# Ten instead of seven seven-product groups, with running results kept in PSUM, in a four-branch decoder layer on one Trainium2 core

## The chip, the cores and the metric

The kernel runs as one program on 1 core of one Trainium2 chip. Its time is the device time of one execution in microseconds (us); the figure quoted is the median over runs. One execution is recorded by the hardware profiler; its rows give start, duration and waits of every instruction on TensorE (PE; PEld is its weight load), VectorE (DVE), ScalarE (ACT), GpSimd (POOL) and on the DMA queue of SyncE (SP).

## The reference, cut to what matters

One layer with a batch of 1, 256 tokens and a model width of 2048, all in float32. The input is normalised and projected to some 22,900 columns; four branches of width 1024 (two masked attentions, a short convolution, a cross-attention) follow; each branch's result is gated and projected, weighted by a sigmoid gate of the input, and summed; one output projection and a final norm follow.

```
xn = rms_norm(x, ln_g)
(a_q, a_k, a_v, a_g, c_b, c_c, c_h, c_g, s_q, s_k, s_v, s_g, m_q, m_g,
 i_q, i_k, i_w, r_a, r_c, r_s, r_m) = [xn @ w for w in cols]
...
y_m = memory_attention(...) * silu(m_g)          # and y_a, y_c, y_s in the same way
merged = (sigmoid(r_a) * (y_a @ w_branch[0]) + sigmoid(r_c) * (y_c @ w_branch[1])
          + sigmoid(r_s) * (y_s @ w_branch[2]) + sigmoid(r_m) * (y_m @ w_branch[3]))
out = rms_norm(x + merged @ w_out, final_g)
```

The gates r_a, r_c, r_s, r_m are each a product of 256 tokens x 2048 by 2048 x 2048; so is the output projection.

## The kernel before, in words

**Three matmuls for one.** Every float32 weight is split into `hi` (a rounded copy, made by ACT) and `lo` (the rest, a subtraction on DVE), and the activations are kept in the same two parts; one exact product is hi*hi + hi*lo + lo*hi, that is three matmuls in the fast float32r form (`products`, `products_t`). A block of 1024 weight columns per partition thus costs one ACT cast (L104) and one DVE subtraction (L105), and 12 matmuls of 512 columns where both halves of the tokens use it. `hi` and `lo` rotate over 4 buffers each; raw weights come by 1 MB DMAs on the SP queue into 4 `raw` buffers.

**Two kinds of projection.** `project_t` keeps weights as the stationary operand and streams the 256 tokens of `x_hl` (256 columns per matmul, tiles `acc`). `project` keeps 128 tokens stationary and streams 512 weight columns, for token half 0 and 1 in turn (tiles `r`, `w`, `v`, `o`): 16 chunks of 128 inputs x 2 token halves x 3 = 96 matmuls for 512 output columns.

**By halves.** Two neighbouring blocks of 512 output columns need 192 matmuls by `project`. `by_halves` takes the first 8 of the 16 input chunks as a 2 x 2 block product (2 token halves, 2 groups of 4 chunks, 2 column blocks) and forms it with seven products instead of eight (the Strassen-Winograd form); the other 8 chunks are added plainly. A product is 4 chunks x 3 = 12 matmuls, so a group has 180. The weights' differences (`b12 - b11` and so on) are made by DVE, in place in the raw tiles; sums of token blocks (`x_sums`) are made once by `sums_of`. In the group before, the products `m1`, `m5`, `m6`, `m7` go to PSUM banks of their own and DVE joins them in SBUF (L248, L249, L254, L255); eight PSUM reads by DVE in all. A scheduler fixes one order of instructions per engine before the program runs; at run time each engine goes through its list in order and waits on semaphores.

**Where groups are used.** Memory branch M, selection branch S, attention branch A: the second half (`j = 1`) of the branch's gate columns; convolution branch C: both halves; and the value projections S_V and A_V: seven groups. The other three gate halves and the output projection go by `project`. The order of work is: M, indexer, S (S_Q, S_K, S_V, attention beside S_G, gates and branch products), A in the same way, C, output blocks 0 to 4 (512, 512, 512, 256, 256 columns) and the final norm.

**Where tiles stand.** Pools are laid one after the other in each partition. Counting the tile sizes in that order, `x_hl` starts 32 bytes past a multiple of 256, `x_sums` too; `y`, `raw`, `hi` and `lo` start 96 bytes past one.

Of the kernel before, what the change touches and what calls it, by code (L numbers as in the profile page):

```python
# [9 lines left out]
F32 = mybir.dt.float32  # L10
# [5 lines left out]
P = 128  # L16
# [21 lines left out]
SECTIONS_N = [(S_V, W), (A_V, W), (R_0, 4 * D)]  # L38
# [6 lines left out]
TOPK = 64  # L45


@with_exitstack
def hybrid_kernel(ctx, tc, x, xT, mem, memT, ln_g, mem_ln_g, w_t, w_n, w_idx, conv_w, conv_b, w_mem_k, w_mem_v,
# [26 lines left out]
    cb = const.tile([P, 8], F32, name="cb")  # L76
    nc.gpsimd.dma_start(out=g_x, in_=ln_g)
# [79 lines left out]
    def products(o, ah, al, hi, lo, start, stop):  # L157

        nc.tensor.matmul(o, lhsT=ah, rhs=hi, start=start, stop=False)  # L159
        nc.tensor.matmul(o, lhsT=ah, rhs=lo, start=False, stop=False)  # L160
        nc.tensor.matmul(o, lhsT=al, rhs=hi, start=False, stop=stop)  # L161
# [60 lines left out]
    def by_halves(srcs, act, sums, nat, done):  # L222
# [3 lines left out]
        (n00, n10), (n01, n11) = ([part(nat, t, n) for t in range(2)] for n in range(2))  # L226

# [5 lines left out]

        b11 = quarter(srcs[0], 0)
# [30 lines left out]
        product(y, a(1, 0), b21, True, False)
        for k0 in (8, 12):
            plain((y, x), act, srcs[0], k0, (False, False), (k0 == 12,) * 2)
        for t, (o, i) in enumerate(((n00, y), (n10, x))):
            nc.vector.tensor_add(o, i, o)
            done(t, 0, o, False)  # L270
# [26 lines left out]
    def columns(c0, nat, done, halved, srcs=None):  # L297
# [416 lines left out]
```

## Time and profile before

| | |
|---|---|
| median of 3 runs | 1399.0 us (1398.69 to 1400.92) |
| the profiled execution's own time | 1398.06 us |
| its span, first to last instruction | 1396.3 us |
| PE busy | 1380.4 us, 99% of the span |
| DVE busy | 933.4 us, 67% |
| ACT busy | 729.2 us, 52% |
| granted TensorE clock, mean | 0.997 of full speed |

The span leaves 1.8 us of the profiled execution's time outside. Matmuls overlap in the pipeline, so PE counts as busy even where they follow each other more slowly than they could; the distance from one matmul's start to the next tells more than the busy share.

### The profile page before, as it was taken

What the parts mean: (1) busy time and instruction counts of PE and PEld (TensorE: products, weight loads), DVE (VectorE), ACT (ScalarE), POOL (GpSimd) and SP (SyncE); (2) the same over time, 40 slices, a digit from 0 to 9 for tenths busy, and PEclk for the clock granted to TensorE, in tenths of its full rate; (3) what the DMA queues carried; (4) which work ended last, traced back from release to release, by engine and by line L of the source; (5) the groups of instructions that cost most, each with busy time, mean ns of one, the idle gap of its engine ahead of it and who ended that gap; (6) DMA issues with size and microseconds to landing.
All of it is one profiled execution on the core that took longest, in us unless ns stands there. A gap on an engine that the chain in (4) does not pass through costs nothing.

```text
span 1396.3 us, 21263 instructions
## 1 busy us (share of the span) xinstructions
PE 1380.4 (99%) x8796; PEld 1243.9 (89%) x8796; DVE 933.4 (67%) x1123; ACT 729.2 (52%) x991; POOL 11.0 (1%) x25
## 2 busy tenths in 40 slices
PE   9999999999999999999999999999999999999997
PEld 9998998789998898878999899878999998878887
DVE  7687764774848884596546885487547558787654
ACT  7663675453445684354445585445343345545443
POOL 1000000000000000000000000000000000000000
PEclk9999999999999999999999999999999999999999
DMA  9774545375554735537553746537555654736551
GB/s 343 291 271 173 191 156 180 128 266 189 172 197 133 254 128 183 189 135 247 188 193 133 243 150 211 182 125 266 183 181 187 225 192 148 265 130 241 183 197 73
DMA packets 49969, 269.49 MB, mean 193 GB/s; under 512 B 6656, under 2 KB 17456, under 8 KB 19024
## 3 DMA queue, kind: packets, MB, share of 16 engines
q1 hardware_dynamic: 48960, 264.03, 55.0%
q0 software_dynamic: 624, 3.31, 0.6%
q8 instruction: 69, 1.13, 0.3%
q10 hardware_dynamic: 288, 0.79, 0.1%
q14 instruction: 28, 0.23, 0.0%
HBM read 265.88 MB, written 2.10 MB: 192 GB/s over the span
## 4 chain that ended last, share of the span: by engine, by line
PE 85%; DVE 8%; DMA 3%; issue 2%; ACT 2%; SPq 0%; POOLq 0%; POOL 0%; DVEq 0%; ACTq 0%
PE acc L138 13%; PE acc L140 13%; PE acc L139 13%; DVE lo L105 5%; PE w L160 4%; PE w L161 4%; PE w L159 4%; PE r L159 4%; PE r L161 4%; PE r L160 4%; PE o L160 2%; PE o L161 2%; PE o L159 2%; DMA raw<-in_w_n 1%; PE y L160 1%
## 5 line engine op out<-in xcount | busy, mean ns | idle before, releaser
L105 DVE TENSOR_TENSOR lo<-raw,hi 128x1024 fp32r<-128x1024 f32 (+1 forms) x538 | 640.0, 1202 | 416.5 <-ACT hi L104 414.4
L104 ACT CAST hi<-raw 128x1024 fp32r<-128x1024 f32 (+1 forms) x538 | 552.2, 1032 | 547.8 <-PE acc L139 196.4
L139 PE MATMUL acc<-x_hl,hi 128*128 128x256 f32 x1520 | 426.0, 280 | 0.0
L138 PE MATMUL acc<-x_hl,hi 128*128 128x256 f32 x1520 | 425.4, 280 | 0.5 <-ACT qt L155 0.5
L140 PE MATMUL acc<-x_hl,lo 128*128 128x256 f32 x1520 | 425.8, 280 | 0.0
L140 PEld LDWEIGHTS acc<-x_hl,lo 128*128 128x128 f32 x1520 | 288.1, 190 | 0.1
L138 PEld LDWEIGHTS acc<-x_hl,hi 128*128 128x128 f32 x1520 | 284.8, 187 | 0.9 <-ACT qt L155 0.7
L139 PEld LDWEIGHTS acc<-x_hl,hi 128*128 128x128 f32 x1520 | 284.8, 187 | 0.2
L159 PE MATMUL w<-hi,y 128*128 128x512 f32 x256 | 99.9, 390 | 0.0
L161 PE MATMUL w<-hi,y 128*128 128x512 f32 x256 | 99.7, 389 | 0.0
L160 PE MATMUL w<-lo,y 128*128 128x512 f32 x256 | 99.6, 389 | 0.0
L159 PE MATMUL r<-hi,x_hl 128*128 128x512 f32 x248 | 98.3, 396 | 0.0
L161 PE MATMUL r<-hi,x_hl 128*128 128x512 f32 x248 | 97.9, 395 | 0.0
L160 PE MATMUL r<-lo,x_hl 128*128 128x512 f32 x248 | 97.6, 394 | 0.0
L159 PEld LDWEIGHTS w<-hi,y 128*128 128x128 f32 x256 | 48.1, 188 | 10.0
L161 PEld LDWEIGHTS w<-hi,y 128*128 128x128 f32 x256 | 48.1, 188 | 10.0
L160 PEld LDWEIGHTS w<-lo,y 128*128 128x128 f32 x256 | 48.1, 188 | 9.9
L161 PEld LDWEIGHTS r<-hi,x_hl 128*128 128x128 f32 x248 | 46.7, 188 | 10.6
L160 PEld LDWEIGHTS r<-lo,x_hl 128*128 128x128 f32 x248 | 46.7, 188 | 10.4
L159 PEld LDWEIGHTS r<-hi,x_hl 128*128 128x128 f32 x248 | 46.9, 189 | 10.2
L161 PE MATMUL o<-hi,mt 128*128 128x512 f32 (+1 forms) x160 | 55.3, 347 | 0.0
L160 PE MATMUL o<-lo,mt 128*128 128x512 f32 (+1 forms) x160 | 55.1, 346 | 0.0
(246 smaller groups left out, 1860.7 us busy)
## 6 DMA issues: line engine op xcount, KB each, us to landing
raw<-in_w_t SPq DMA_DIRECT2D x92, 1024.0 KB, 5.0
raw<-in_w_n SPq DMA_DIRECT2D x80, 1024.0 KB, 4.9
raw<-in_w_branch SPq DMA_DIRECT2D x32, 1024.0 KB, 5.3
raw<-in_w_out SPq DMA_DIRECT2D x16, 1024.0 KB, 4.8
raw<-in_w_mem_k SPq DMA_DIRECT2D x8, 1024.0 KB, 6.4
raw<-in_w_mem_v SPq DMA_DIRECT2D x8, 1024.0 KB, 5.5
raw<-in_w_t SPq DMA_DIRECT2D x16, 256.0 KB, 5.9
raw<-in_memT SPq DMA_DIRECT2D x2, 1024.0 KB, 8.8
```

The costliest lines, as they stand in the source:

```text
L104: nc.scalar.copy(out=hi, in_=src)
L105: nc.vector.tensor_sub(out=lo, in0=src, in1=hi.bitcast(F32))
L138: nc.tensor.matmul(o, lhsT=hi, rhs=a[:, 0], start=(k == 0), stop=False)
L139: nc.tensor.matmul(o, lhsT=hi, rhs=a[:, 1], start=False, stop=False)
L140: nc.tensor.matmul(o, lhsT=lo, rhs=a[:, 0], start=False, stop=(k == nk - 1))
L159: nc.tensor.matmul(o, lhsT=ah, rhs=hi, start=start, stop=False)
L160: nc.tensor.matmul(o, lhsT=ah, rhs=lo, start=False, stop=False)
L161: nc.tensor.matmul(o, lhsT=al, rhs=hi, start=False, stop=stop)
```

## The change

It does five things. (1) `by_halves` is rewritten: the bank `u` takes the product a11*b11, is copied out by ACT (L253), goes on accumulating s1*h1, is copied out again (L265), goes on with s2*h2, is copied out a third time (L268), and then takes the plain part; bank `m` likewise takes s0*h1, is copied (L260) and goes on. DVE adds only four times at the end (`finish`, L247), ACT copies four times instead of once. (2) The weight differences go to tiles `held` of their own, in the room of `kt` and `vv` for gates and of `y` elsewhere; raw tiles are no longer overwritten. (3) The gates of S and A at `j = 0` and output blocks 1 and 2 become groups: ten in all; the output pair needs sums of `mt`, made by one more `sums_of` (two raw buffers, `m_sums` in the room of `x_sums`). (4) Tiles move: a 224-byte tile `fill`, 256 more bytes in each `hi` and `lo` tile, and 448 more in `u` put `x_hl`, `x_sums`, `mt`, `y`, `raw`, `hi` and `lo` on multiples of 256 bytes; a `hi` or `lo` used as the stationary operand begins 64 bytes later. (5) `yt` has one buffer instead of two.

```
+STATIONARY = 64
+    fill = const.tile([P, 56], F32, name="fill")
+    nc.gpsimd.memset(fill, 0.0)
...
-    def parts_tiles(w=NB, c=NB):
-        return [spl.tile([P, 2 * NB], F32R, name=n, tag=n).rearrange("p (k c) -> p k c", c=w)[:, :, :c]
-                for n in ("hi", "lo")]
+    def parts_tiles(w=NB, c=NB, place=0):
+        i = place // 4
+        return [spl.tile([P, 2 * NB + 64], F32R, name=n, tag=n)[:, i:i + 2 * NB]
+                .rearrange("p (k c) -> p k c", c=w)[:, :, :c] for n in ("hi", "lo")]
...
-                hi, lo = parts_tiles(w, c)
+                hi, lo = parts_tiles(w, c, STATIONARY if w == TB else 0)
...
-    def by_halves(srcs, act, sums, nat, done):
+    def by_halves(srcs, act, sums, nat, done, room):
...
+        held = [big.tile([P, 8 // len(room) * NB], F32, name="held", tag=r) for r in room]
+        h1, h2 = (v.rearrange("p (k c) -> p k c", c=NB) for v in
+                  (held if len(room) == 2 else (held[0][:, :4 * NB], held[0][:, 4 * NB:])))
...
         b11 = quarter(srcs[0], 0)
-        m1 = bank("m", tag)
-        product(m1, a(0, 0), b11, True, True)
-        nc.scalar.copy(out=n00, in_=m1)
-        z, r = bank("z", other), bank("r", other)
-        plain((z, r), act, srcs[1], 8, (True, True), (False, False))
+        u = bank("u", tag)
+        product(u, a(0, 0), b11, True, True)
+        nc.scalar.copy(out=n00, in_=u)
+        x, y = bank("x", other), bank("y", other)
+        plain((y, x), act, srcs[0], 8, True, False)
         b12 = quarter(srcs[1], 0)
-        nc.vector.tensor_sub(out=b11, in0=b12, in1=b11)
-        m5 = bank("m", tag)
-        product(m5, s(0), b11, True, True)
+        nc.vector.tensor_sub(out=h1, in0=b12, in1=b11)
+        m = bank("m", tag)
+        product(m, s(0), h1, True, True)
+        nc.scalar.copy(out=n11, in_=m)
+        plain((y, x), act, srcs[0], 12, False, False)
         b22 = quarter(srcs[1], 4)
-        nc.vector.tensor_sub(out=b11, in0=b22, in1=b11)
-        m6 = bank("m", tag)
-        product(m6, s(1), b11, True, True)
-        nc.vector.tensor_add(n10, m6, n00)
-        nc.vector.tensor_add(n01, m5, n10)
-        plain((z, r), act, srcs[1], 12, (False, False), (False, True))
-        nc.vector.tensor_sub(out=b12, in0=b22, in1=b12)
-        m7 = bank("m", tag)
-        product(m7, s(2), b12, True, True)
-        nc.vector.tensor_add(n10, m7, n10)
-        nc.vector.tensor_add(n11, m7, n01)
-        product(z, s(3), b22, False, True)
...
+        nc.vector.tensor_sub(out=h1, in0=b22, in1=h1)
+        product(u, s(1), h1, False, True)
+        nc.scalar.copy(out=n01, in_=u)
+        nc.vector.tensor_sub(out=h2, in0=b22, in1=b12)
+        product(u, s(2), h2, False, True)
+        nc.scalar.copy(out=n10, in_=u)
+        product(m, s(3), b22, False, False)
+        plain((m, u), act, srcs[1], 8, False, False)
         b21 = quarter(srcs[0], 4)
...
+        nc.vector.tensor_sub(out=h1, in0=b21, in1=h1)
+        product(x, a(1, 1), h1, False, True)
+        finish(x, 1, 0)
+        plain((m, u), act, srcs[1], 12, False, True)
+        product(y, a(1, 0), b21, False, True)
+        finish(m, 0, 1)
+        finish(u, 1, 1)
+        finish(y, 0, 0)
...
-    finish(BR_S, S_G, q, (False, True))
+    finish(BR_S, to_gate(S_G, q))
...
-    finish(BR_A, A_G, q, (False, True))
+    finish(BR_A, to_gate(A_G, q))
...
+    sums_of(lambda k0, n: mt[:, k0:k0 + n], m_sums[0])
...
+        yield from block(0)
+        got = []
+        nat = nat_tile("no")
+        by_halves([w_out[1], w_out[2]], lambda k: mt[:, k], m_sums[0], nat,
+                  lambda t, n, src, psum: got.append((1 + n, t, src)), ("y",))
+        yield from got
+        for n in range(3, last + 1):
+            yield from block(n)
```

The order that the scheduler fixes, at three places, all in the gate group of branch S at `j = 1`. First PE, before: the end of product `m5` (its bank is `m_5988`) and the beginning of `m6` (`m_6012`).

```order
L161 MATMUL m_5988<-hi_5999,x_sums_1518 128x512
L159 MATMUL m_5988<-hi_5999,x_sums_1518 128x512
L160 MATMUL m_5988<-lo_6000,x_sums_1518 128x512
L161 MATMUL m_5988<-hi_5999,x_sums_1518 128x512
L159 MATMUL m_6012<-hi_6013,x_sums_1518 128x512
L160 MATMUL m_6012<-lo_6014,x_sums_1518 128x512
L161 MATMUL m_6012<-hi_6013,x_sums_1518 128x512
```

The two products that need fresh differences stand side by side there. PE after, at the second and third products that bank `u` takes (`u_5950`); `m_6011` is bank `m`:

```order
L167 MATMUL u_5950<-lo_6081,x_sums_1520 128x512
L168 MATMUL u_5950<-hi_6080,x_sums_1520 128x512
L166 MATMUL m_6011<-hi_6113,x_sums_1520 128x512
L166 MATMUL u_5950<-hi_6092,x_sums_1520 128x512
L167 MATMUL u_5950<-lo_6093,x_sums_1520 128x512
L168 MATMUL u_5950<-hi_6092,x_sums_1520 128x512
L166 MATMUL u_5950<-hi_6092,x_sums_1520 128x512
```

One matmul for bank `m` now stands between the last one that adds s1*h1 to `u` and the first that adds s2*h2; the two plain runs stand ahead, one on either side of s0*h1.

DVE before, around the difference that `m6` needs (L245); `lo_6014` and `lo_6024` are its rests, and L499 adds up branch products of the gate half before:

```order
L499 TENSOR_TENSOR merged_2561<-merged_2561,sig_5495 128x512
L105 TENSOR_TENSOR lo_5990<-raw_5925,hi_5989 128x1024
L105 TENSOR_TENSOR lo_6000<-raw_5925,hi_5999 128x1024
L499 TENSOR_TENSOR merged_2561<-merged_2561,sig_5495 128x512
L245 TENSOR_TENSOR raw_5925<-raw_6009,raw_5925 128x2048
L105 TENSOR_TENSOR lo_6014<-raw_5925,hi_6013 128x1024
L105 TENSOR_TENSOR lo_6024<-raw_5925,hi_6023 128x1024
```

The difference L245 reads the tile that `lo_6000` has just read, and `lo_6014` follows it at once. DVE after, at the same step (L263 is the difference that L245 was, L266 the one for h2):

```order
L266 TENSOR_TENSOR held_5947<-raw_6067,raw_6008 128x2048
L110 TENSOR_TENSOR lo_6013<-held_5946,hi_6012 128x1024
L110 TENSOR_TENSOR lo_6023<-held_5946,hi_6022 128x1024
L110 TENSOR_TENSOR lo_6036<-raw_6033,hi_6035 128x1024
L263 TENSOR_TENSOR held_5946<-raw_6067,held_5946 128x2048
L110 TENSOR_TENSOR lo_6052<-raw_6033,hi_6051 128x1024
L110 TENSOR_TENSOR lo_6071<-held_5946,hi_6070 128x1024
L110 TENSOR_TENSOR lo_6081<-held_5946,hi_6080 128x1024
L110 TENSOR_TENSOR lo_6093<-held_5947,hi_6092 128x1024
L272 TENSOR_TENSOR held_5946<-raw_6167,held_5946 128x2048
```

The rests for s0*h1 (`lo_6013`, `lo_6023`) and a plain block now stand ahead of the difference L263, one plain block behind it, and h2 is made earlier. ACT after, around the second copy (L265) and the third (L268) out of `u_5950`; the other rows are casts:

```order
L109 CAST hi_6092<-held_5947 128x1024
L109 CAST hi_6102<-held_5947 128x1024
L109 CAST hi_6113<-raw_6067 128x1024
L265 COPY sig_5945<-u_5950 128x512
L109 CAST hi_6123<-raw_6067 128x1024
L109 CAST hi_6135<-raw_6133 128x1024
L268 COPY sig_5945<-u_5950 128x512
L109 CAST hi_6151<-raw_6133 128x1024
```

One cast stands ahead of the second copy, two between it and the third.

## Rows read from the trace of the kernel before

**Rows 1.** The page: span, busy time of the engines, the granted TensorE clock in 40 slices.

```profile
span 1396.3 us, 21263 instructions
PE 1380.4 (99%) x8796; PEld 1243.9 (89%) x8796; DVE 933.4 (67%) x1123; ACT 729.2 (52%) x991; POOL 11.0 (1%) x25
...
PEclk9999999999999999999999999999999999999999
```

**Rows 2.** Busy time by stretch: the seven groups, each from its first matmul to the first of the next stage. Columns: start and end, length, busy time and instruction count of PE, PEld, DVE, ACT, POOL, granted clock, DMA share, GB/s.

```profile
261.30:304.05 42.75, 41.90 (x182) 33.52 (x181) 37.68 (x35) 23.97 (x25) 0.00 (x0) 1.00 0.60 207
432.88:476.01 43.13, 42.91 (x194) 35.04 (x193) 38.32 (x40) 26.54 (x32) 0.00 (x0) 1.00 0.60 208
598.46:643.61 45.15, 43.59 (x181) 34.79 (x180) 38.99 (x37) 24.36 (x25) 0.00 (x0) 0.96 0.58 198
755.83:798.99 43.16, 42.94 (x195) 35.04 (x194) 38.21 (x40) 26.52 (x32) 0.00 (x0) 1.00 0.60 207
921.38:965.28 43.90, 42.27 (x182) 33.49 (x180) 38.80 (x37) 23.99 (x25) 0.00 (x0) 1.00 0.59 203
1167.96:1210.39 42.43, 42.09 (x182) 33.50 (x181) 37.36 (x35) 26.12 (x29) 0.53 (x1) 1.00 0.67 236
1233.06:1276.38 43.32, 42.38 (x182) 33.42 (x180) 38.16 (x36) 23.98 (x25) 0.00 (x0) 1.00 0.60 208
sum 303.84, PE 298.07 PEld 238.80 DVE 267.52 ACT 175.47 POOL 0.53; mean PE 42.58 PEld 34.11 DVE 38.22 ACT 25.07 POOL 0.08
```

**Rows 3.** The same view of the three stretches that become groups: the gate of S at `j = 0`, that of A, and output blocks 1 and 2.

```profile
531.88:576.68 44.80, 44.80 (x194) 36.30 (x193) 20.83 (x18) 20.49 (x23) 0.00 (x0) 1.00 0.55 182
854.80:899.60 44.80, 44.80 (x194) 36.30 (x193) 20.82 (x18) 20.50 (x23) 0.00 (x0) 1.00 0.60 205
1322.81:1366.76 43.95, 43.95 (x194) 36.06 (x192) 24.42 (x25) 19.31 (x24) 0.00 (x0) 1.00 0.52 177
```

**Rows 4.** The same view of four other stretches: a branch product of S (tiles `w`, 96 matmuls of 512 columns), and three stretches of `project_t` (256 columns): most of S_Q and S_K (576 matmuls), A_Q and A_K (768), C_C to C_G (1,536).

```profile
576.68:598.46 21.78, 21.78 (x97) 18.02 (x96) 13.78 (x13) 9.03 (x10) 0.00 (x0) 1.00 0.48 166
367.60:432.88 65.28, 65.28 (x578) 65.28 (x577) 40.23 (x58) 28.90 (x38) 0.00 (x0) 1.00 0.54 186
665.37:755.83 90.46, 90.46 (x770) 90.45 (x769) 43.89 (x39) 38.05 (x49) 0.00 (x0) 1.00 0.53 181
987.05:1167.96 180.91, 180.91 (x1538) 180.91 (x1536) 100.96 (x115) 73.94 (x83) 0.54 (x1) 1.00 0.55 189
```

**Rows 5.** The instructions in order of time around the end of `m5` in the S group. Columns: start, duration, engine, line and operation; in brackets the idle time before and what ended it.

```profile
606.92 2.28 DVE L245 TENSOR_TENSOR raw<-raw 128x2048 f32<-128x2048 f32 x1
...
609.23 0.39 PE L161 MATMUL m<-hi,x_sums 128*128 128x512 f32 x1
609.32 3.89 ACT L104 CAST hi<-raw 128x1024 fp32r<-128x1024 f32 x4 [1.69 <-DVE raw L245]
610.40 2.36 DVE L105 TENSOR_TENSOR lo<-raw,hi 128x1024 fp32r<-128x1024 f32 x2 [1.19 <-ACT hi L104]
...
610.42 0.51 PE L159 MATMUL m<-hi,x_sums 128*128 128x512 f32 x1 [0.81 <-ACT hi L104]
...
611.68 0.50 PE L160 MATMUL m<-lo,x_sums 128*128 128x512 f32 x1 [0.75 <-DVE lo L105]
```

**Rows 6.** The same view at the copy of `m1` in the first C group.

```profile
1170.50 0.39 PE L161 MATMUL m<-hi,x_hl 128*128 128x512 f32 x1
...
1170.92 0.59 ACT L237 COPY sig<-m 128x512 f32<-128x512 f32 x1 [0.28 <-PE m L161]
```

**Rows 7.** The same view where PE waits for ACT in the attention of S.

```profile
509.47 0.35 ACT L104 CAST pt<-pp 128x256 fp32r<-128x256 f32 x1
...
509.88 0.38 PE L353 MATMUL yp<-pt,part 128*128 128x256 f32 x1 [0.38 <-ACT pt L104]
```

**Rows 8.** Groups of instructions by line and shape on DVE: count | busy us, mean ns of one | idle time before them and what ended it.

```profile
L105 DVE TENSOR_TENSOR lo<-raw,hi 128x1024 fp32r<-128x1024 f32 x518 | 626.9, 1223 | 403.8 <-ACT hi L104 402.0
L241 DVE TENSOR_TENSOR raw<-raw 128x2048 f32<-128x2048 f32 x7 | 16.0, 2293 | 0.2
...
L499 DVE TENSOR_TENSOR merged<-merged,sig 128x512 f32<-128x512 f32 x24 | 15.6, 684 | 0.0
```

**Rows 9.** The same view of the casts on ACT.

```profile
L104 ACT CAST hi<-raw 128x1024 fp32r<-128x1024 f32 x518 | 540.6, 1050 | 538.1 <-PE acc L139 190.0 <-PE w L161 95.1 <-PE r L161 74.1
```

**Rows 10.** The chain that ended last, in the first C group: start, duration, what.

```profile
1183.00 4.92 DMA raw<-in_w_n
1187.94 1.15 DVE raw L261
```

**Rows 11.** The DMA issues of the `project` and `by_halves` weights of the input: count, KB each, us from issue to landing.

```profile
raw<-in_w_n SPq DMA_DIRECT2D x80, 1024.0 KB, 4.9
```

More of the change, by code (lines that the diff above doesn't have):

```diff
@@ L37 @@
 SECTIONS_T = [(c, W) for c in (M_Q, M_G, S_Q, S_K, S_G, A_Q, A_K, A_G, C_C, C_H, C_B, C_G)]
[L38 removed]
+SECTIONS_N = [(c, W) for c in (S_V, A_V)] + [(R_0, 4 * D)]
 FIRST = {}
@@ L155, in copy_t, with products @@
             nc.scalar.activation(out=dst[:, j], in_=a[:rows], func=func)
[L157 to L161, printed above, removed]
+    def products(o, ah, al, hi, lo, start, stop, **kw):
+        nc.tensor.matmul(o, lhsT=ah, rhs=hi, start=start, stop=False, **kw)
+        nc.tensor.matmul(o, lhsT=ah, rhs=lo, start=False, stop=False, **kw)
+        nc.tensor.matmul(o, lhsT=al, rhs=hi, start=False, stop=stop, **kw)
     def project(src, act, name, t_outer=False):
@@ L209, in product @@
             al = a(k)
-            products(o, al[:, 0], al[:, 1], hi, lo, start and k == 0, stop and k == 3)
+            products(o, al[:, 0], al[:, 1], hi, lo, start and k == 0, stop and k == 3, skip_group_check=True)
     def plain(o, act, src, k0, start, stop):
@@ L295, in x_act, with columns @@
         return x_hl[:, k]
-    def columns(c0, nat, done, halved, srcs=None):
+    def columns(c0, nat, done, halved, srcs=None, room=("y",)):
         if srcs is None:
@@ L301, in columns @@
         if halved:
-            return by_halves(srcs, x_act, x_sums, nat, done)
+            return by_halves(srcs, x_act, x_sums, nat, done, room)
         for n in range(2):
@@ L479, in gate_columns @@
         sig = nat_tile("sig")
-        columns(None, sig, through(sig, AF.Sigmoid), halved, [w_n[FIRST[R_0] + 4 * b + 2 * j + n] for n in range(2)])
+        columns(None, sig, through(sig, AF.Sigmoid), halved, [w_n[FIRST[R_0] + 4 * b + 2 * j + n] for n in range(2)],
+                room=("kt", "vv"))
         return sig
@@ L582, in hybrid_kernel, with finish @@
     memory_attention(q, k, v)
-    def finish(b, gate, val, halved, after=None):
-        y = to_gate(gate, val)
+    def finish(b, y, halved=(True, True), after=None, last=None):
         for j in range(2):
-            merge(b, j, gate_columns(b, j, halved[j]), y, after)
-    finish(BR_M, M_G, q, (False, True))
+            sig = gate_columns(b, j, halved[j])
+            if j == 1 and last is not None:
+                last()
+            merge(b, j, sig, y, after)
+    finish(BR_M, to_gate(M_G, q), halved=(False, True))
     mask_s = indexer(*indexer_parts())
@@ new lines, in blocks_of, with block @@
+    def blocks_of():
+        def block(n):
+            c0, c = blocks[n]
+            acc = project(w_out[c0 // NB][:, :, c0 % NB:c0 % NB + c], lambda k: mt[:, k], "o", t_outer=(n == last))
+            return ((n, t, acc[t]) for t in range(2))
+        yield from block(0)
[6 more added lines that the diff above has]
+            yield from block(n)
@@ new lines, in hybrid_kernel @@
+    for n, t, src in blocks_of():
+        c0, c = blocks[n]
+        ns = slice(c0, c0 + c)
+        o = xr[t][:, ns]
+        nc.vector.tensor_add(o, src, o)
+        nc.scalar.activation(out=junk[:, t, :c], in_=o, func=AF.Square, accum_out=ss[:, t, n:n + 1])
+        if n < last:
+            nc.vector.tensor_mul(o, o, fg[:, ns])
+        if n == last - 1:
+            nc.vector.tensor_reduce(out=pre[:, t:t + 1], in_=ss[:, t, :last], axis=AX.X, op=ALU.add)
+            nc.vector.tensor_scalar(pre[:, t:t + 1], pre[:, t:t + 1], 1.0 / D, EPS, op0=ALU.mult, op1=ALU.add)
+        if n == last:
+            nc.vector.tensor_scalar(var[:, t:t + 1], ss[:, t, n:], 1.0 / D, pre[:, t:t + 1], op0=ALU.mult,
+                                    op1=ALU.add)
+            nc.gpsimd.tensor_tensor(out=inv[:, t:t + 1], in0=var[:, t:t + 1], in1=mhalf[:, 0:1], op=ALU.pow)
+            nc.vector.tensor_mul(o, o, fg[:, ns])
+            for eng, cs in ((nc.vector, slice(0, 512)), (nc.scalar, slice(512, 1280)), (nc.vector, slice(1280, D))):
+                o = xr[t][:, cs]
+                if eng is nc.vector:
+                    nc.vector.tensor_scalar(o, o, inv[:, t:t + 1], None, op0=ALU.mult)
+                else:
+                    nc.scalar.activation(out=o, in_=o, func=AF.Copy, scale=inv[:, t:t + 1])
+                (nc.scalar if eng is nc.scalar else nc.sync).dma_start(out=out[t * P:(t + 1) * P, cs], in_=o)
```

68 lines of the change are left out of this document (22 added, 46 removed).

## The prediction

> **What bounds the kernel now.** I read the page first: PE is busy for 99% of the span at full granted clock, DVE for 67%, ACT for 52% [rows 1]. So nearly every microsecond is set by how many matmuls PE issues, how far apart they start, and the few places where it waits. The change touches all three, so I priced stretches, not the whole.
>
> The stretches of the seven groups [rows 2] show what the present form is worth. A group has 180 matmuls where the plain form has 192, yet takes 42.4 to 45.2 us against 44.8 for a plain gate half and 43.95 for two output blocks [rows 3]: 303.84 us for seven. About 2.7 us of that is attention work interleaved in the two value groups (12 to 13 PE instructions more than in the others [rows 2], at 0.113 us), so a group is (303.84 - 2.7)/7 = 43.0 us. A branch product gives 21.78/96 = 0.2269 us from matmul to matmul [rows 4], by which 180 would take 40.8 us: 2.2 us per group are lost. The order of time shows where: after `m5` PE starts nothing from 609.23 to 610.42 and from 610.42 to 611.68, first for ACT's cast, then for DVE's rest, because the difference L245 (2.28 us) could begin only when the rests for `m5` were done [rows 5]. DVE is busy 38.2 of 43.4 us there [rows 2], against 20.8 of 44.8 in a plain half [rows 3]. In the C group the chain goes through a weight transfer, 4.92 us, into L261 [rows 10]: the raw tiles that hold differences are missing for prefetch. So a group is a PE stretch that DVE, almost full, and the raw buffers make wait.
>
> **The change, part by part.**
>
> *Work on DVE in a group.* Before: 22 rests at 1.223 us, 4 differences at 2.29 and 8 PSUM additions at 0.684 [rows 8] = 26.9 + 9.2 + 5.5 = 41.6 us. After: 4 additions, so 38.8. Three copies more go to ACT, 0.59 us each [rows 6]; with 22 casts of 1.05 us [rows 9] it has 22 x 1.05 + 4 x 0.59 = 25.5 us of some 42, which hides them.
>
> *The order.* Before, the two products with fresh differences stand side by side: 5.4 us of matmuls against two differences and four rests. After, plain runs of 24 matmuls stand on both sides of s0*h1. I went through DVE's new list for the S group at `j = 1`, with time 0 at the group's first matmul. By then `lo_5977` and all before it can be done, since the branch product needs DVE little (13.8 of 21.8 us [rows 4]). Four branch additions, 2.8 us, begin about 0.2 after 0. Then, at the durations above: `lo_5993` done at 4.2, L266 6.5, `lo_6013` 7.7, `lo_6023` 8.9, `lo_6036` 10.2, L263 12.4, `lo_6052` 13.7, `lo_6071` 14.9. PE, at 0.2269 a matmul, wants `lo_5993` at 6.1, `lo_6013` at 8.8, `lo_6036` at 11.3, `lo_6052` at 14.1, `lo_6071` at 16.6. Every one is in time, the tightest by 0.4 us. For what this leaves out (a cast or a buffer somewhat late) I take 0.3 us per group; the bounds are 0 and the 2.2 us lost now.
>
> *Transfers.* Differences leave the raw tiles, so b11 and b12 free theirs early and b21 can be issued several quarters ahead. A quarter lands in 4.9 us [rows 11] and eight of them take about the 42 us of a group; the DMA share of 0.6 [rows 2] leaves room. The 4.9 us link should vanish from the chain; it is part of the 2.2 us, not counted again.
>
> *The wait that the change adds.* Between s1*h1 and s2*h2 on bank `u`, PE must wait for ACT's copy; one matmul for `m` stands between. ACT starts 0.42 us after the start of the last matmul and takes 0.59 [rows 6]; PE follows ACT's end by 0.06 [rows 7]. That is 1.07 us from start to start where two intervals would be 0.45, so 0.61 us; the first matmul after a wait costs 0.12 more (0.51 long against 0.39 [rows 5]): 0.73 us. Queued behind it on PE is everything. One cast stands ahead of this copy on ACT, but its buffer frees six matmuls, 1.4 us, earlier, and it takes 1.05. The other three copies have 12 or more matmuls of another bank as cover; without it each would cost the same 0.73.
>
> *How far apart matmuls start.* Widths equal, `r` starts every 44.80/192 = 0.2333 us, `o` every 43.95/192 = 0.2289, `w` every 0.2269 [rows 3, 4]. In `r` and `o` the stationary tile begins at 32 bytes past a multiple of 256 and the moving one at 96; in `w` both begin at 96. After, all three pairs begin alike, as `w` did. So I take 0.2269 for every 512-column matmul of a group; were it 0.2289 or 0.2333, ten groups would cost 3.6 or 11.5 us more. That the place does it is an inference from three pairs. For 256 columns the relative place stays (64 bytes apart) and I take no change, although the same tiles run at 65.28/576 = 0.1133 in one stretch and 90.46/768 = 0.1178 in others [rows 4]. The Trainium skill (SBUF — State Buffer, Specifications) says that SBUF is read in lines of 16 bytes and that a crossing to a new line costs; all these starts, before and after, are multiples of 16, so by it the move does nothing and my sum would be 1386 to 1394. It leaves the spread between `r` and `w` unexplained, so I keep the rows.
>
> *The sum.* A group: 180 x 0.2269 + 0.73 + 0.3 = 41.87 us; ten: 418.7, and 2.7 for attention. Before, the same work: 303.84 + 44.80 + 44.80 + 43.95 = 437.4. Saved: 437.4 - 421.4 = 16.0 us.
>
> *Costed at nothing.* The sums of `mt`: DVE 2 x 1.22 + 8 x 0.68 = 7.9 us, spread over the last branch product and output block 0, about 43 us of PE in which DVE is busy for 63% by the branch product in [rows 4]; without that cover up to 7.9 us. Additions and squares of blocks 1 and 2 fall into blocks 3 and 4. One `yt` buffer: a chain under 3 us every 11. `fill`: one small memset on POOL ahead of its first DMA, in a start set by weight transfers. The tail is the same. Attention that now reaches into the first groups of S and A keeps its PE work.
>
> From the profiled execution's 1398.06 us (span 1396.3) to **1382 us**; the median of the runs stands 0.9 higher, and I leave that out.
>
> **Rivals.**
>
> *Nothing but one column per cycle (faster still).* If the new places also took away what lies above one column per cycle at the granted full clock (2.4 GHz: 0.1067 and 0.2133 us), some 5,100 matmuls of 256 columns would save 0.0066 and some 3,000 of 512 columns 0.0136, 75 us together: about 1307. No stretch here comes near it, and `w`, with equal places, doesn't either. The Trainium skill (TensorE: Matmul & The Clock Gate, "Wait — 56ns, not 53.3ns?") states just that pace plus 2.5 ns per matmul; by it 0.2158, which the rows do not bear out.
>
> *The 256-column stretches fall to their lower pace.* The two long ones at 0.1178 hold 768 + 1,536 matmuls [rows 4]; at 0.1133 they save 2,304 x 0.0045 = 10 us: 1372. For it: the same tiles have run so; against: the relative place is kept.
>
> *ACT comes late to the copy.* If the cast ahead of it has just begun, another 1.05 us per group: 10.5 in all, 1392.
>
> *DVE stays the bound (the other side).* If the differences make PE wait as now, a group takes 43.0, the copy's 0.73 comes on top, and ten are 437.3 + 2.7 = 440: 2.6 us more than before, 1401; with every group like the slowest [rows 2], 1420. For it: DVE still needs 38.8 of 42 us, with a margin of 0.4 at one place. Against: 2.8 us less DVE work and the new order. It decides from (437.4 - 2.7)/10 = 43.5 us per group on.
>
> That the matmuls are not removed is no rival: three groups more have 36 fewer by construction.
>
> **How the numbers follow.** The measurement of this kernel cannot tell less than about 0.2% (2.8 us) from no change. Forecast (1375 to 1389): 0.55. Lower pace at 256 columns (1364 to 1375): 0.20. One column per cycle or part of it (below 1364): 0.05. Late copies (1389 to 1395): 0.07. DVE the bound (1394 to 1420): 0.13, of which 0.02 is below 1396, 0.05 within 0.2%, 0.06 above. So faster 0.89, same 0.05, slower 0.06. The range 1364 to 1396 leaves out the fast end and most of the last case; the likeliest case alone spans 1375 to 1389.
>
> **What would show it.** Right: gate groups of 41.5 to 42.5 us; in each one PE wait of about 0.4 to 0.5 us idle named after ACT's copy L265, and no wait of over 0.5 us for a rest or cast of `held`; `r`, `x`, `y`, `m`, `u`, `o` starting every 0.227 us; no weight transfer on the chain inside groups. Wrong: groups of 43 us and more with PE waiting for `lo` from `held`; 512-column matmuls still 0.229 to 0.233 apart; 256-column stretches at another pace than 0.1133 to 0.1178; a copy that waits behind casts.

## The result and the profile after

The changed kernel takes **1380.42 us** (median; 1380.36 to 1383.67), the kernel before 1399.96 in the same runs: a ratio of 0.9866, 95% interval 0.9848 to 0.9884. Predicted were 1382.0, range 1364 to 1396. The profiled execution of after is the longest of its four (1383.67 us, span 1381.5), so its rows add up to a little more than the median. One of the four executions of experiment e11 ran at a mean granted clock of 0.556 and took 2283.5 us; the figures of e11 below are those of the other three.

The page of after, to be held against [rows 1]: span, busy time, and the chain that ended last by engine.

```profile
span 1381.5 us, 21305 instructions
PE 1368.3 (99%) x8760; PEld 1241.8 (90%) x8760; DVE 974.9 (71%) x1147; ACT 770.6 (56%) x1050; POOL 11.2 (1%) x26
...
PE 97%; ACT 1%; issue 0%; DMA 0%; DVE 0%; POOLq 0%; POOL 0%; DVEq 0%; SPq 0%; ACTq 0%
```

The same line of the chain in the page of before:

```profile
PE 85%; DVE 8%; DMA 3%; issue 2%; ACT 2%; SPq 0%; POOLq 0%; POOL 0%; DVEq 0%; ACTq 0%
```

DVE is busier than before over the whole, because three more groups have differences and more rests to make and `mt` has its sums, but DVE and DMA have fallen to 0% of the chain. What is on it beside PE is ACT.

Busy time by stretch: the ten groups, columns as in [rows 2]. These stretches answer to [rows 2] and [rows 3] together.

```profile
264.21:305.75 41.54, 41.15 (x181) 33.71 (x180) 34.34 (x29) 25.77 (x29) 0.00 (x0) 1.00 0.54 189
434.73:477.76 43.03, 42.64 (x195) 35.03 (x193) 35.11 (x35) 28.00 (x35) 0.00 (x0) 1.00 0.51 181
533.35:575.45 42.10, 41.70 (x186) 34.19 (x185) 34.10 (x29) 29.25 (x35) 0.00 (x0) 1.00 0.54 191
597.21:638.77 41.56, 41.17 (x181) 33.72 (x180) 35.09 (x31) 25.56 (x29) 0.00 (x0) 1.00 0.54 189
...
sum 419.62, PE 415.69 PEld 340.76 DVE 348.40 ACT 271.32 POOL 1.75; mean PE 41.57 PEld 34.08 DVE 34.84 ACT 27.13 POOL 0.17
```

Groups without attention take 41.54 to 41.57 us, every one the same; the two with most attention 43.03 and 43.05, the first gate groups of S and A, into which a little attention reaches, 42.10 and 42.08. In [rows 2] the same work took 42.43 to 45.15. The sum is 419.6 where before it was 437.4.

Around the second copy out of bank `u`, in the gate group of S at `j = 1`, in order of time (columns as in [rows 5]):

```profile
616.03 0.39 PE L168 MATMUL u<-hi,x_sums 128*128 128x512 f32 x1
...
616.25 0.45 PE L166 MATMUL m<-hi,x_sums 128*128 128x512 f32 x1
616.45 0.58 ACT L265 COPY sig<-u 128x512 f32<-128x512 f32 x1 [0.30 <-PE u L168]
...
617.09 0.50 PE L166 MATMUL u<-hi,x_sums 128*128 128x512 f32 x1 [0.39 <-ACT sig L265]
...
617.42 0.39 PE L167 MATMUL u<-lo,x_sums 128*128 128x512 f32 x1
```

From 616.03 to 617.09 are 1.06 us where two intervals would be 0.45, and the next matmul follows after 0.33 instead of 0.227: 0.71 us. PE's waits over the span, with total, count and longest, name the same copy ten times:

```profile
PE u L166 <- ACT sig L265: 2.7, 7, 0.4
PE warm L96 <- DVE table L92: 1.2, 1, 1.2
PE u L166 <- ACT vv L265: 0.8, 2, 0.4
PE u L166 <- ACT no L265: 0.4, 1, 0.4
...
```

The two left out are 0.3 and 0.2 us, at the start and in the attention. No wait of PE names a rest or cast of `held`. The 256-column stretches after the change: M_Q's rest and the keys of the memory, S_Q and S_K, A_Q and A_K, C_C to C_G; the last three answer to [rows 4].

```profile
28.75:96.94 68.19, 68.19 (x582) 68.19 (x581) 48.37 (x54) 45.12 (x66) 2.33 (x2) 1.00 0.77 286
369.45:434.73 65.28, 65.28 (x579) 65.28 (x577) 40.55 (x58) 28.85 (x38) 0.00 (x0) 1.00 0.57 196
...
660.53:750.99 90.46, 90.46 (x770) 90.46 (x769) 43.97 (x39) 38.18 (x49) 0.00 (x0) 1.00 0.56 189
976.80:1157.70 180.90, 180.90 (x1537) 180.90 (x1536) 100.97 (x115) 74.07 (x83) 0.00 (x0) 1.00 0.56 188
```

Three kept their length to 0.01 us. The first took 65.80 us in the profile of before. Output blocks 3 and 4, behind the last group (192 matmuls of 256 columns), took 21.86 there, 0.1133 from matmul to matmul:

```profile
28.49:94.29 65.80, 65.80 (x581) 65.80 (x581) 48.12 (x54) 45.65 (x66) 2.33 (x2) 1.00 0.80 291
...
1366.76:1388.62 21.86, 21.86 (x193) 21.72 (x191) 12.03 (x22) 8.76 (x16) 0.68 (x1) 1.00 0.07 25
```

After, these two blocks take 22.62, that is 0.1178:

```profile
1351.27:1373.89 22.62, 22.62 (x193) 22.57 (x191) 14.96 (x26) 9.09 (x18) 0.68 (x1) 1.00 0.07 26
```

### The profile page after: what moved, and what is told of

It reads as the page before. It is cut to its first block, busy times and chain, and to the rows that moved or that the text cites. A ratio compares the mean times of both kernels' runs of the same rounds, so it can differ in the third digit from the quotient of the medians.

```text
span 1381.5 us, 21305 instructions
## 1 busy us (share of the span) xinstructions
PE 1368.3 (99%) x8760; PEld 1241.8 (90%) x8760; DVE 974.9 (71%) x1147; ACT 770.6 (56%) x1050; POOL 11.2 (1%) x26
## 4 chain that ended last, share of the span: by engine, by line
PE 97%; ACT 1%; issue 0%; DMA 0%; DVE 0%; POOLq 0%; POOL 0%; DVEq 0%; SPq 0%; ACTq 0%
PE acc L147 14%; PE acc L145 14%; PE acc L146 14%; PE w L167 4%; PE w L168 4%; PE w L166 4%; PE u L166 3%; PE u L168 3%; PE u L167 3%; PE m L168 3%; PE m L167 3%; PE m L166 2%; PE y L168 2%; PE y L167 2%; PE y L166 2%; PE x L166 2%
## 5 line engine op out<-in xcount | busy, mean ns | idle before, releaser
L110 DVE TENSOR_TENSOR lo<-raw,hi 128x1024 fp32r<-128x1024 f32 (+1 forms) x476 | 567.7, 1199 | 357.2 <-ACT hi L109 354.9
L109 ACT CAST hi<-raw 128x1024 fp32r<-128x1024 f32 (+1 forms) x476 | 489.1, 1030 | 456.1 <-PE acc L146 203.0
L110 DVE TENSOR_TENSOR lo<-held,hi 128x1024 fp32r<-128x1024 f32 x80 | 95.0, 1221 | 5.7 <-ACT hi L109 5.5
L109 ACT CAST hi<-held 128x1024 fp32r<-128x1024 f32 x80 | 82.9, 1055 | 22.9 <-PE x L168 18.8
L166 PE MATMUL y<-hi,x_hl 128*128 128x512 f32 x108 | 42.4, 393 | 0.0
L168 PE MATMUL u<-hi,x_hl 128*128 128x512 f32 x108 | 42.3, 391 | 0.0
L167 PE MATMUL u<-lo,x_hl 128*128 128x512 f32 x108 | 42.1, 390 | 0.0
L166 PE MATMUL u<-hi,x_hl 128*128 128x512 f32 x108 | 42.1, 390 | 0.0
L168 PE MATMUL y<-hi,x_hl 128*128 128x512 f32 x108 | 42.1, 390 | 0.0
L167 PE MATMUL y<-lo,x_hl 128*128 128x512 f32 x108 | 42.1, 390 | 0.0
```

The source lines that it names most:

```text
L109: nc.scalar.copy(out=hi, in_=src)
L110: nc.vector.tensor_sub(out=lo, in0=src, in1=hi.bitcast(F32))
L168: nc.tensor.matmul(o, lhsT=al, rhs=hi, start=False, stop=stop, **kw)
```

## The experiments

The questions were: what does each part give (places, form of the group, room for differences, three more groups), is the copy wait worth what its rows say, and what sets the distance between matmuls. Ratios are to the kernel before in the same runs; the ten groups are the sum of their stretches (in e3 some 9 matmuls of the last group lie behind its stretch).

| kernel | median us | ratio, 95% interval | ten groups us |
|---|---|---|---|
| changed kernel | 1380.4 | 0.9866 (0.9848 to 0.9884) | 419.62 |
| e1, old places | 1382.4 | 0.9887 (0.9872 to 0.9902) | 423.12 |
| e2, seven groups | 1386.3 | 0.9915 (0.9901 to 0.9930) | |
| e3, old form | 1395.9 | 0.9975 (0.9964 to 0.9986) | 430.46 |
| e4, places only | 1395.6 | 0.9975 (0.9966 to 0.9985) | |
| e5, all shifted by 32 | 1382.2 | 0.9885 (0.9865 to 0.9906) | |
| e6, stationary at 0 | 1398.7 | 1.000 (0.9991 to 1.001) | |
| e7, copy covered | 1373.7 | 0.9824 (0.9803 to 0.9844) | 412.13 |
| e8, differences in raw | 1394.2 | 0.9971 (0.9960 to 0.9982) | 431.36 |
| e9, stationary at 128 | 1389.0 | 0.9922 (0.9907 to 0.9937) | |
| e10, stationary at 32 | 1381.6 | 0.9868 (0.9852 to 0.9885) | |
| e11, all moving at 64 | 1369.4 | 0.9790 (0.9771 to 0.9809) | |
| e12, branch products at 64 | 1365.0 | 0.9757 (0.9743 to 0.9770) | |

**e3: the old form of the group in everything else that is new.** `by_halves`, `product` and `plain` are those of before.

> The changed kernel with by_halves, product and plain as before the change (four banks joined by DVE, differences in the raw tiles, s0 and s1 products side by side), in all ten groups and at the new places. Theory: the waits for DVE and the raw tiles come back, 1.7 to 2.2 us per group in place of 0.72: a group of 42.5 to 43.0 us, the sum 10 to 15 us longer, 1390 to 1395; waits named after hi and lo of raw inside m5 to m7. Rival (the new form gains nothing, and the places and the three groups are all): no copy wait, so 7 us less, 1373 to 1381.

1395.9 us, just above the range of the theory: the new form is worth 15 us. Busy time by stretch of two groups, and of 3.2 us inside the second:

```profile
597.75:642.59 44.84, 42.27 (x181) 33.42 (x180) 38.85 (x37) 24.21 (x25) 0.00 (x0) 1.00 0.58 198
917.05:962.61 45.56, 43.82 (x182) 34.60 (x181) 39.12 (x37) 24.07 (x25) 0.00 (x0) 0.96 0.57 194
...
930.20:933.40 3.20, 3.15 (x8) 2.47 (x9) 3.20 (x3) 2.29 (x3) 0.00 (x0) 0.53 0.00 0
```

The same kernel where products `m5` and `m6` meet in the first of the two:

```profile
606.21 2.28 DVE L252 TENSOR_TENSOR raw<-raw 128x2048 f32<-128x2048 f32 x1
...
608.41 0.39 PE L168 MATMUL m<-hi,x_sums 128*128 128x512 f32 x1
609.70 0.50 PE L166 MATMUL m<-hi,x_sums 128*128 128x512 f32 x1 [0.91 <-ACT hi L109]
610.96 0.50 PE L167 MATMUL m<-lo,x_sums 128*128 128x512 f32 x1 [0.76 <-DVE lo L110]
```

It is the stall of [rows 5]: difference late, then cast, then rest. In the second group it costs more than the wait: eight matmuls follow at 0.43 us, granted clock 0.53, that is near the lower level of 1.2 GHz. So what the group loses to DVE can cost the clock too, and [rows 2] has one such stretch at 0.96.

**e4: the new places alone, in the kernel before.** `fill`, larger `hi`, `lo` and `u`, the start at 64, one `yt`.

> The kernel before with the new places alone (fill, larger hi and lo tiles with the start 64 bytes later for a stationary one, larger u, one yt buffer). Theory: 512-column matmuls on x_hl, x_sums and mt go from 0.229 to 0.2333 us apart to 0.2267. The steady part of that is 7 us over the whole kernel; what falls into the seven groups is partly taken back by waits for DVE: 4 to 7 us less, 1393 to 1396, plain gate halves at 43.5 instead of 44.8 us. Rival (no effect of places): 1400.

1395.6 us, inside the range, though 3 us less than before where 4 to 7 were expected. A plain gate half and the sum of its seven groups:

```profile
534.45:578.00 43.55, 43.55 (x194) 36.04 (x193) 20.80 (x18) 20.60 (x23) 0.00 (x0) 1.00 0.56 185
...
sum 302.97, PE 295.68 PEld 237.30 DVE 266.96 ACT 175.38 POOL 0.53; mean PE 42.24 PEld 33.90 DVE 38.14 ACT 25.05 POOL 0.08
```

The plain half falls from 44.80 [rows 3] to 43.55, 192 x 0.2267. The seven groups fall only from 303.84 [rows 2] to 302.97: there PE's faster pace becomes waiting for DVE. e3 has the same places and three groups more, and the same time: in the old form the three extra groups gave nothing in the total. Two of them did gain (41.65 and 41.67 us in e3 against 43.55 for the plain half here); the third, output blocks 1 and 2, took 43.09 with some 9 matmuls still to come.

**e8: differences written over raw tiles, the new order kept.**

```
-        held = [big.tile(...) for r in room]
-        h1, h2 = ...
...
+        h1 = b11
         nc.vector.tensor_sub(out=h1, in0=b12, in1=b11)
...
+        h2 = b12
         nc.vector.tensor_sub(out=h2, in0=b22, in1=b12)
```

> The changed kernel with the differences written over raw tiles as before the change (h1 over b11, h2 over b12; no tiles held), all else, the order of products included, as changed. Theory (the order of products removes the waits for DVE; the room for differences is needed for the prefetch): with two of four raw buffers held, transfers come late once per group, 1 to 2 us each: 1390 to 1400, waits of PE that go back to a weight transfer. Rival (the order alone does it, the tiles held give nothing): 1380 to 1383, with groups of 41.6 us.

1394.2 us: 14 us of the gain are gone with the room. Five groups still take 41.55, so the loss does not come in every group as the theory had it: it is in those that follow a 256-column stretch (47.39, 46.00 and 43.14, and 43.55 and 43.50 for the two with most attention, which take 43.03 and 43.05 in the changed kernel). The instructions around the stall in the worst one, then 3.2 us behind it and the whole stretch:

```profile
544.56 2.29 DVE L261 TENSOR_TENSOR raw<-raw 128x2048 f32<-128x2048 f32 x1 [2.70 <-DMA raw<-in_w_n]
...
548.07 0.50 PE L166 MATMUL u<-hi,x_sums 128*128 128x512 f32 x1 [1.93 <-ACT hi L109]
550.25 0.50 PE L167 MATMUL y<-lo,x_hl 128*128 128x512 f32 x1 [1.68 <-DVE lo L110]
```

```profile
551.40:554.60 3.20, 3.20 (x10) 2.41 (x9) 2.20 (x2) 0.66 (x1) 0.00 (x0) 0.50 0.67 215
534.61:582.00 47.39, 43.39 (x182) 34.76 (x181) 34.32 (x30) 28.86 (x34) 0.00 (x0) 0.96 0.51 177
```

`b11` and `b12` hold two of four raw buffers, DVE waits 2.70 us for a weight transfer, PE loses 3.6 us and then runs at granted clock 0.50. The new order without the room and the old form without it (e3) are 1.7 us apart, and by their ratios (0.9971 and 0.9975, with intervals that overlap almost whole) they can't be told apart. In the new order the room is worth 14 us. What the room would give to the old order was not tried.

**e2: seven groups instead of ten.** `halved=(False, True)` for S and A, output blocks 1 and 2 by `project`, no `m_sums`.

> The changed kernel with seven groups instead of ten: the gates of S and A at j = 0 and output blocks 1 and 2 go by project again, without the sums of mt. Theory: a group saves 12 matmuls of 0.2267 us and pays 0.72 us for the wait for ACT's copy, 2.0 us net; three groups are worth 6.0 us: 1386.4, with the plain halves at 192 x 0.2267 = 43.5 us. Rival (a group is worth no more than a plain half, as before the change, since DVE makes it wait): 1380 to 1381.

1386.3 us: three groups are worth 5.9. A plain half and a group of this kernel:

```profile
531.05:574.60 43.55, 43.55 (x194) 36.05 (x193) 20.72 (x18) 21.96 (x24) 0.00 (x0) 1.00 0.56 186
596.36:637.91 41.55, 41.16 (x182) 33.70 (x180) 35.08 (x31) 25.59 (x29) 0.00 (x0) 1.00 0.54 190
```

The difference is 2.0 us, three times.

**e7: the copy covered.**

```
         nc.scalar.copy(out=n01, in_=u)
         nc.vector.tensor_sub(out=h2, in0=b22, in1=b12)
+        product(m, s(3), b22, False, False)
         product(u, s(2), h2, False, True)
         nc.scalar.copy(out=n10, in_=u)
-        product(m, s(3), b22, False, False)
```

> The changed kernel with the product s3*b22 into bank m moved ahead of s2*h2 in by_halves, so that six matmuls of another bank stand between the last one of s1*h1 and the first of s2*h2 on bank u, where one stands now. Theory (each group loses 0.72 us to the wait for ACT's second copy): all ten waits gone, 7.2 us less, 1373, groups of 40.9 us. Rival (the wait moves on, to the third copy or to a rest of held that is then late, or DVE makes it wait): 1378 to 1382 with another wait named in its place.

1373.7 us, 6.7 less than the changed kernel, which it beats. All its PE waits, one group, and the sum of the ten:

```profile
PE warm L96 <- DVE table L92: 1.2, 1, 1.2
PE yp L371 <- ACT pt L109: 0.2, 1, 0.2
```

```profile
594.05:634.85 40.80, 40.80 (x182) 33.80 (x180) 35.04 (x31) 25.60 (x29) 0.00 (x0) 1.00 0.55 193
...
sum 412.13, PE 412.13 PEld 341.51 DVE 347.79 ACT 271.31 POOL 1.75; mean PE 41.21 PEld 34.15 DVE 34.78 ACT 27.13 POOL 0.18
```

40.80 is 180 x 0.2267; 0.76 per group. No other wait took its place.

**e1: the old places in the changed kernel**, the instructions of PE, DVE and ACT in the same order.

> The changed kernel with its tiles put back: no fill tile, hi and lo tiles of the old size with no start 64 bytes later, u of the old size. x_hl, x_sums, m_sums and mt stand at 32 past a multiple of 256 bytes again, y, raw, hi and lo at 96; the order of instructions on PE, DVE and ACT is that of the changed kernel. Theory (the place sets the pace of 512-column matmuls): those on x_hl and x_sums (1,812) and on mt and m_sums (276) go from 0.2267 us apart back to 0.229 to 0.2333, which adds 4 to 12 us: 1385 to 1392; those on y (branch products) keep 0.2267, since y, hi and lo still start alike. Rival (nothing changes, since all starts are multiples of 16): 1380.4, with 512-column matmuls 0.2267 apart.

1382.4 us; its interval overlaps that of the changed kernel, so by the total alone the places can't be told from nothing. The stretches can: a group, the 256-column start, and the sum of the ten groups.

```profile
594.19:636.12 41.93, 41.53 (x181) 33.72 (x180) 35.15 (x31) 25.55 (x29) 0.00 (x0) 1.00 0.53 187
27.95:93.67 65.72, 65.72 (x583) 65.72 (x581) 48.03 (x54) 45.65 (x67) 2.33 (x2) 1.00 0.80 303
...
sum 423.12, PE 419.05 PEld 340.78 DVE 348.96 ACT 271.22 POOL 1.75; mean PE 41.90 PEld 34.08 DVE 34.90 ACT 27.12 POOL 0.17
```

The groups lose 3.5 us, and the start is 2.5 shorter than in the profile of after. For the 512-column matmuls the theory holds in kind (41.93 less the copy wait's 0.74 is 180 x 0.2288), with less in the groups than its 4 to 12 us; its 1385 to 1392 was missed. The start is another matter (e5).

**e5: every place shifted by 32 bytes**, relative places as changed (`fill` left out).

> The changed kernel without the fill tile: every tile that matmuls read stands 32 bytes past a multiple of 256, a weight tile used as the stationary operand 64 bytes further, so that all places relative to each other are those of the changed kernel. In the profile of the changed kernel 256-column matmuls on m16a, m16b (the keys of the memory) and in the last two output blocks start 0.1178 us apart, in that with the old places 0.1133. Theory A (only relative places count, what differed at 256 columns is chance from one execution to the next): 512-column matmuls at 0.2267, 256-column ones at either pace, 1380 to 1384. Theory B (the absolute place sets the 256-column pace): 512-column ones at 0.2267 and 256-column ones on m16a, m16b and mt at 0.1133 again, 3 to 6 us less: 1375 to 1378.

1382.2 us. The start and a group:

```profile
28.45:94.23 65.78, 65.78 (x581) 65.78 (x581) 48.39 (x54) 45.76 (x66) 2.33 (x2) 1.00 0.81 298
594.53:636.08 41.55, 41.16 (x182) 33.70 (x180) 35.09 (x31) 25.59 (x29) 0.00 (x0) 1.00 0.54 188
```

The group is that of the changed kernel: the shift changes nothing for 512 columns, only the relation of the two operands counts (theory A, as far as this run goes). The start is at the lower level again, but it is so in e2 too (28.40 to 94.06 us), whose places there are those of the changed kernel; so it is not the absolute place that decides it.

**e6, e9, e10: the stationary tile 0, 128 or 32 bytes from the moving one** at 256 columns (`STATIONARY` = 0 in the changed kernel; 128 and 32 in e7, to be held against 1373.7).

> The changed kernel with the stationary hi and lo tiles at the same place as the moving operand, on a multiple of 256 bytes (the start 64 bytes later left out). Theory (operands that start alike go at the lower of the two distances, whatever the width): all 256-column matmuls 0.1133 apart, the 5,100 of them up to 0.0045 each where they were at 0.1178: 15 to 20 us less, 1361 to 1366. Rival (the same place is wrong for 256 columns, which the 64 bytes are there for): 0.1178 or more everywhere, 5 us longer or more, 1385 and up. Rival (no effect at 256 columns): 1380 to 1384.

> The version with the copy covered (s3*b22 ahead of s2*h2), and the stationary weight tiles 128 bytes instead of 64 past the place of the moving operand; order and all else as there. At equal places 256-column matmuls started 0.1199 us apart, at 64 bytes 0.1133 to 0.1178. Theory A (the further apart the starts, the better, until 0.1133 holds everywhere): 14 to 17 us less than 1373.7, 1357 to 1360. Theory B (64 is as good as another distance that isn't 0, and the rest is chance from stretch to stretch): 1370 to 1377. Theory C (128 is like 0): 0.1199 everywhere, 1389 and up.

> The same with the stationary tiles 32 bytes past the place of the moving operand. Theory A (further apart is better): between the paces at 0 and 64, 0.118 to 0.120 everywhere, 1377 to 1389. Theory B (any distance but 0 does): 1370 to 1377. Theory C (a small distance is better): below 1368.

1398.7, 1389.0 and 1381.6 us. The stretch of A_Q and A_K (768 matmuls) in e6, which takes 92.17 us in e9 likewise:

```profile
668.68:760.83 92.15, 92.15 (x770) 92.15 (x768) 43.95 (x39) 38.13 (x49) 0.00 (x0) 1.00 0.55 186
```

and in e10:

```profile
662.17:753.05 90.88, 90.88 (x770) 90.88 (x768) 43.96 (x39) 38.21 (x49) 0.00 (x0) 1.00 0.56 188
```

0.1200, 0.1200 and 0.1183 us per matmul, against 0.1178 at 64 bytes. My theory for e6 (alike is best at any width) was wrong, and its first rival came out: the distance that is best at 512 columns is, with 128 bytes, the worst at 256. In e9 theory C came out in the time (128 is like 0, 1389 and up), and theory A, further apart is better, falls with it, although e10 by itself lies in A's range. Of the four distances tried, 64 gives the shortest time.

**e11: the moving weight tiles of 512 columns also at 64 bytes** (in e7).

```
-                hi, lo = parts_tiles(w, c, STATIONARY if w == TB else 0)
+                hi, lo = parts_tiles(w, c, STATIONARY)
...
-            hi, lo = parts_tiles()
+            hi, lo = parts_tiles(place=STATIONARY)
```

> The version with the copy covered, with the weight tiles that are the moving operand of 512-column matmuls also 64 bytes past the place of the stationary ones (which stand on multiples of 256); 256-column matmuls keep their 64 bytes. Theory (512-column matmuls go at the lower distance only where both operands start alike): all 3,000 of them, the branch products on y included, back from 0.2267 to 0.229 to 0.2333, 7 to 20 us more than 1373.7: 1381 to 1394. Rival (it is the absolute place of x_hl, not the relation): 0.2267 kept, 1372 to 1376.

1369.4 us, faster than e7, on neither theory's account. A branch product, A_Q with A_K, and a group:

```profile
636.98:658.95 21.97, 21.97 (x98) 18.03 (x96) 14.13 (x16) 9.58 (x10) 0.00 (x0) 1.00 0.65 217
658.95:746.01 87.06, 87.06 (x769) 87.06 (x768) 43.94 (x39) 38.20 (x49) 0.00 (x0) 1.00 0.57 195
...
595.78:636.98 41.20, 41.20 (x182) 33.81 (x181) 35.13 (x31) 25.53 (x29) 0.00 (x0) 1.00 0.54 191
```

The 512-column part went as the theory has it: 0.2289 in branch product and group here, and 0.2333 in those of M, whose group takes 42.00 us. But the 256-column stretch, whose tiles and order are untouched, fell from 0.1178 to 0.1134.

**e12: only the branch products' weight tiles at 64 bytes** (in e7). `project` and `split_weights` hand `place` on to the tiles.

```
...
-            acc = project(w_branch[b, n], lambda k: y[:, k], "w")
+            acc = project(w_branch[b, n], lambda k: y[:, k], "w", place=STATIONARY)
```

> The version with the copy covered, with the weight tiles of the branch products alone (768 matmuls of 512 columns on y) 64 bytes past the place of the stationary y; all other 512-column matmuls start alike, 256-column ones keep their 64 bytes. With every 512-column matmul 64 bytes apart the long 256-column stretches of A_Q, A_K and C_C to C_G, laid out as ever, went at 0.1133 instead of 0.1178, and each of them follows a branch product. Theory (a 256-column stretch keeps the pace that the work ahead of it leaves, and a branch product 64 bytes apart leaves the lower one): 2,304 x 0.0045 = 10 us less for the two stretches, 768 x 0.0023 to 0.0034 = 1.8 to 2.6 us more for the branch products: 1365 to 1367. Rival (the pace comes from elsewhere, the whole of the 512-column work or chance): the stretches stay at 0.1178, and the branch products make it 1375 to 1377.

**1365.0 us**, the fastest of all: a ratio of 0.9757 to the kernel before. Branch product, A_Q with A_K, C_C to C_G, and the start:

```profile
635.98:657.97 21.99, 21.99 (x97) 18.03 (x96) 14.19 (x16) 9.63 (x10) 0.00 (x0) 1.00 0.64 214
657.97:745.03 87.06, 87.06 (x770) 87.06 (x768) 43.94 (x39) 38.19 (x49) 0.00 (x0) 1.00 0.57 195
969.09:1143.18 174.09, 174.09 (x1537) 174.09 (x1536) 100.52 (x115) 74.12 (x83) 0.00 (x0) 1.00 0.57 194
...
28.86:97.06 68.20, 68.20 (x582) 68.20 (x581) 48.35 (x54) 45.30 (x66) 2.33 (x2) 1.00 0.77 285
```

The two long stretches are 3.4 and 6.8 us shorter than in e7, the eight branch products 0.23 longer each, and the theory came out. At 64 bytes 256-column matmuls have two levels, and here the work ahead chose the lower one. The profile of before fits: A_Q follows a branch product with equal places as in e7 and is at 0.1178 likewise. So does the tail, output blocks 3 and 4, in all eleven profiles with 64 bytes: 0.1133 where the 512-column matmuls ahead of it stand 64 bytes apart (before, e1, e11), 0.1178 where they start alike (the other eight, this one among them). It is no rule for every stretch: the start, with no such work ahead, ran at either level in kernels with the same places there, and in e11 the 256-column matmuls beside the memory attention kept 0.118 behind `v` matmuls 64 bytes apart, 0.2333 us from start to start. What carries the pace over is open.

## Why the prediction was right, and where its steps were not

**The ten groups.** Predicted 421.4 us, measured 419.6; saved 17.8 where 16.0 were predicted. A group without attention was to be 41.87 and is 41.55: 180 x 0.2267 and 0.74 beside, of which the rows give 0.71 to the copy, predicted at 0.73. The 0.3 for "a cast or a buffer somewhat late" is not there; that term was too large by 3 us over ten groups. Attention went the other way: taken at 2.7 us, it is 4.1 by the rows (43.03, 43.05, 42.10 and 42.08 against 41.55), because it reaches into the first gate groups of S and A; so part of the agreement is two misses against each other. e7 took the copy wait away and got 7.5 us from the groups (419.62 to 412.13), so this price was real and not merely a row.

**DVE's list.** Every rest came in time, the tightest of my walk (0.4 us) included; the rival in which DVE stays the bound did not occur; e3 shows that its waits stay with the old form. DVE is busy 34 to 36 us in a group's stretch, not 38.8: in the group of S at `j = 1` the first difference and some rests are made before the stretch begins.

**Transfers.** I counted the room for differences inside the 2.2 us per group and put the gain down to the order of products. The weights are the other way round: by e8 the order without the room keeps 1.7 of the 15.4 us that lie between the old form (e3) and the new, and 1.7 is not clear of the noise. What I had not priced is what a late transfer costs: PE idles over 3 us and then runs at the lower clock for another 3.

**Three more groups.** 5.9 us by e2, where the rows at the predicted prices give 3 x (192 x 0.2269 - 41.87) = 5.1.

**Places.** That a 512-column matmul starts every 0.2267 us when both operands start alike was inferred from three pairs; e1 (apart: 0.229), e5 (alike, elsewhere: 0.2267) and e11 (apart again: 0.2289) confirm it as a matter of the relation of the two. It is worth 3.5 us in the new groups, the lower of my two bounds (3.6 and 11.5), and 1.25 us in a plain gate half. My pairs hid one thing: `r` starts every 0.2333 us in the halves of S and A, but in M's half of before every 0.2289 (98 matmuls in 22.44 us, from 217.09), with the same places; at 512 columns, too, one relation has two paces. The Trainium skill (SBUF — State Buffer, Specifications) gives lines of 16 bytes and a penalty at a crossing; I had used that as the rule by which the move does nothing. The rows do not bear it out as the whole account: all places tried are multiples of 16, and the distances differ by up to 6%.

**256 columns.** "I take no change" held for the three long stretches to 0.01 us. In the start it did not in the profiled execution (65.80 to 68.19); these 2.4 us may be most of the 3.3 by which it is longer than the other three, of which no rows exist. "The tail is the same" failed as well: its 192 matmuls went from 0.1133 to 0.1178, 0.8 us in all, behind a group that now starts its operands alike (see e12). The step that failed in both is that the relative place alone fixes the pace. I named the two levels and gave the lower one 0.20 as something that might come by itself; it did not come in this change, and e12 shows what it is worth in the two long stretches: 10.2 us, and about 9 in the total.

**The sum of total.** The ten groups save 17.8 of the profiled execution's time, the start gives back 2.4, and the whole moved from 1398.06 to 1383.67, by 14.4. Of the rest (about 1 us) 0.8 is the tail. By the medians it is 19.5 us; so 1382 was near for partly opposite misses, none over about 3 us.

## What to carry to other kernels

Take a stage's loss from matmul count times the best pace seen, then ask for each wait whether it is late work or a held buffer: here a better order was worth nothing clear of the noise until the differences had room of their own. An accumulation that is read out and goes on needs matmuls of another bank behind it (one was too few, six enough); moving one product up was worth more than the three extra groups (7.5 us of the groups' stretches against 6.0). When the engine is at 99% the distance between starts is the next thing to read, stretch by stretch and width by width, and a gain or a loss in it can lie in a stretch that was not touched.

## What the runs showed of the hardware that I had not expected

- The distance between starts of matmuls depends on how far apart in a partition the two operands begin. In A_Q and A_K (256 columns) it is 0.1200 us at 0 (e6) and at 128 bytes (e9), 0.1183 at 32 (e10), and 0.1178 (e7) or 0.1134 (e11, e12) at 64; S_Q and S_K, also at 64, ran at 0.1133 [rows 4]. At 512 columns it is 0.2267 at 0 (e7), and 0.2289 or 0.2333 at 64 ([rows 3], e11). The Trainium skill (TensorE: Matmul & The Clock Gate, Step-by-step: what each phase is for) says that the streamed and the stationary operand have read ports of their own, independent of each other. No run here looks at ports, but the relation of the two starts moves the pace in all of them. Why is open.
- At 64 bytes the long stretches stay at one of two levels, which can be set by work ahead of them (e7 against e12: the same 768 matmuls in 90.45 and 87.06 us; the 192 of the tail in 21.86 us before and 22.62 after).
- After two idle times of PE of 1.93 and 1.68 us the granted clock was 0.50 for 3.2 us (e8), after 0.91 and 0.77 us 0.53 in one group of e3, while another group of e3 with 0.91 and 0.76 kept 1.00.
